# Order of the experts on TensorE, one more weight slot, one sum for the last pair and two store queues in a mixture-of-experts layer

## The chip, the core and the metric

The kernel runs on one core of a Trainium2 chip. Its time is the device time of one launch in microseconds (us), and less is better. Five engines share the core's memory: TensorE (PE in the profile, with PEld for loading the stationary operand), VectorE (DVE), ScalarE (ACT), GpSimd (POOL) and SyncE (SP). SP does no arithmetic here, it issues transfers. An engine takes its instructions in the order in which the program lists them, and waits at an instruction until what that one needs is there.

## The reference

One transformer layer on 512 tokens of width 1024, in float32: first `x + hybrid_mixer(rms_norm(x))` (a short convolution, a sparse attention and a gated delta rule, merged by gates), then `x + hier_moe(rms_norm(x))`. The change lies in the second half, whose core is:

```python
def hier_moe(h, w_rg, b_rg, w_re, b_re, w_eg, w_eu, w_ed):
    # a token takes the best of 4 groups, and in it the best 2 of 8 experts
    ...
    def expert_block(args):
        xb, e = args
        return (jax.nn.silu(xb @ w_eg[e]) * (xb @ w_eu[e])) @ w_ed[e]
    ...
    y = yb...[dest] * gate_s[:, None]
    return jax.ops.segment_sum(y, tok_s, num_segments=n_tok)
```

There are 32 experts with two matrices of 1024x512 (gate `w_eg`, up `w_eu`) and one of 512x1024 (down `w_ed`) each, 6.3 MB an expert and 201 MB in all. Every one is read once.

## The kernel before

The mixer, the router and the tables of tokens fill the first 687 us. The rest is the loop `for pair in range(16)` (line 1326), followed by the last expert's down products (lines 1360 to 1382) and a block under `tc.If(any_over > 0)` (line 1386) that runs only when an expert has more than 64 tokens; with this input it does no work.

**A pair** is the experts `pair` and `pair + 16`, with 64 token slots each. `gather` (line 1160) fetches the pair's 128 token rows by index into `xg`; `turned` (line 1114) transposes them on TensorE (`pxg`) and multiplies by the norm's gain on VectorE into `xT`. `ffn_up` (line 1182) makes the gate and up products of one expert side by side in one PSUM tile `pgu` (lines 1185, 1186); ScalarE and VectorE make the activation `act` from it, `turn` transposes that (`pt`, line 1204), and `ffn_down` (line 1222) makes the down products `pd` (line 1228). In every second expert of a pair, the transposes of the other are called in the middle of its products.

**What becomes of `pd`.** For the pairs 0, 1, 11, 12 and 13 (`by_rows`, line 1246) ScalarE copies it and GpSimd scatters it to `yrows` in memory; these rows are fetched during pair 14 (`fetch_rows`, into weight slots), summed and added to the result `x` (`add_rows`, line 1275). For the other pairs `y_parts` (line 1217) makes a rounded half on ScalarE and the rest on VectorE into `y`, and VectorE makes a 0/1 matrix `sel` from the token numbers (line 1213), behind `y_parts` in the program. `combine` lists eight steps, four blocks of 128 tokens by two halves of 512 columns. `combine_step` (line 1280) is `sel` times `y` for each expert of the pair into `pc` (line 1286) and an add into `x` on VectorE (line 1288). Up to four of these steps are called in each `ffn_up` of the next pair.

**Weights.** `wchunk` (line 1073) loads 1 MB chunks, twelve a pair (four for each `ffn_up`, two for each `ffn_down`), all on SP's queue and from the 19th on in program order. They go in turn through 18 slots: chunk n takes the slot of chunk n - 18 when that one's last reader is done. `fetch_rows` takes four slots in the same turn. The last expert's `w_ed` comes as three chunks of 384, 320 and 320 columns.

**The end.** After the last pair's first expert, `combine` is called for that expert alone and its eight steps are run (`combine_rest`, line 1361). Then, for each of the three pieces of columns, come the down products (line 1376), `y_parts`, four combine steps of one expert each, and four stores to the output on SP (`store`, line 1305), one for each block of 128 tokens. The products of the second piece are told to come behind the eight steps of the first expert, those of the third behind the first piece's steps.

**Order on the engines.** The program text is not the order of issue. The kernel is built with `schedule_with_timeline_sim=True`: a planner lists the instructions of each engine by readiness in its own simulated time, with the program's order as priority. `tc.issue_after(ins)` forces a place behind an instruction; `tc.keep_in_program_order` keeps the program's order among those that ask for it. What the planner lists is fixed; on the chip the engine keeps that order whatever comes late.

Of the kernel before, what the change touches and what calls it, by code (L numbers as in the profile page):

```python
# [11 lines left out]
F32 = mybir.dt.float32  # L12
# [8 lines left out]
P = 128  # L21
S = 512
D = 1024
# [5 lines left out]
CAP = 64  # L29
# [70 lines left out]
def kernel(ctx, tc, x, w_in, w_nat, w_small, w_gate, w_branch, w_out, cmp_w1, cmp_w2,  # L100
# [966 lines left out]
    gp = late.enter_context(tc.tile_pool(name="gather", bufs=1))  # L1067
    ep = late.enter_context(tc.tile_pool(name="experts", bufs=1))
    tc.swap_default_side()
    slots = wslots + [(lp, f"{n}{i}") for n in ("hTh", "hTl") for i in range(2)]  # L1070
    nslot, nsel, rows, todo = [0], [0], [], []

    def wchunk(shape, src):
# [10 lines left out]

    gain = PR("nffg")

    def pair_input():
        return gp.tile([P, KT, 2 * CAP], F32, tag="xT", name="xT", bufs=3)

    itab = pair_input().rearrange("p k s -> p (k s)")[:, 0:512].rearrange("p (j c) -> p j c", c=64)  # L1090
    for j, tab in enumerate(islots):
        (nc.scalar if j < 4 else G).dma_start(itab[:, j], tab.rearrange("(p e) c -> p (e c)", p=P))

# [17 lines left out]
                                op0=ALU.mult, op1=ALU.add)  # L1111
                G.tensor_scalar(out=toks[64 * a:64 * a + 64, h], in0=info[hs, :, 0], scalar1=4096.0, scalar2=None, op0=ALU.add)

    def turned(xg):
        xT = pair_input()
        for h in range(2):
            pt = ps_mm.tile([P, 4, P], F32, tag="mm", name="pxg")
            for k in range(4):
                T.transpose(pt[:, k], xg[:, 4 * h + k::KT], ident)
            V.tensor_tensor(out=xT[:, 4 * h:4 * h + 4], in0=pt,  # L1120
                            in1=gain[:, 4 * h:4 * h + 4].unsqueeze(2).to_broadcast([P, 4, P]), op=ALU.mult)
        return xT
# [31 lines left out]
        with tc.issue_after(gathered[0][1]):  # L1154
            tables()

    gathered, moved = [], []


    def gather(pair):  # L1160
# [21 lines left out]
    def ffn_up(xs, wg, wu, info, between=None):  # L1182
        pgu = mpsum("pgu")
        for k in range(KT):
            T.matmul(pgu[0:64], xs(k), wg(k), start=k == 0, stop=k == KT - 1)  # L1185
            ins = T.matmul(pgu[64:128], xs(k), wu(k), start=k == 0, stop=k == KT - 1)  # L1186
            if between and k == 3:
                between()
            if k % 4 == 3:
                combine_step()  # L1190
                combine_step()
        with tc.issue_after(ins.ins):
            rss, gsl = info()
        act = ep.tile([P, 512], F32, tag="act", name="act")
        qk = lambda ap: ap.rearrange("p (q k) -> p k q", k=4)
        at = act[64:128].rearrange("p (k q) -> p k q", k=4)
        A.activation(at, qk(pgu[0:64]), AF.Silu, scale=rss)  # L1197
        V.scalar_tensor_tensor(out=at, in0=qk(pgu[64:128]), scalar=gsl, in1=at, op0=ALU.mult, op1=ALU.mult)  # L1198
        aT = ep.tile([P, 4, CAP], F32, tag="aT", name="aT", bufs=2)

        def turn():
            pt = ps_e.tile([P, 4, CAP], F32, tag="pt", name="pt")
            for k in range(4):
                ins = T.transpose(pt[:, k], act[64:128, k * P:(k + 1) * P], ident[64:128, 64:128])
            V.tensor_copy(aT, pt)
            return ins.ins

        return turn, aT
# [13 lines left out]
    def ffn_down(aT, wd, tok, between=None, to=None):  # L1222
        pd = mpsum("pd")

        def products(ks):
            for k in ks:
                for a in range(2):
                    T.matmul(pd[64 * a:64 * a + 64], aT[:, k], wd(k, a), start=k == 0, stop=k == 3)  # L1228

        products((0, 1))  # L1230
        with tc.issue_after(between()) if between else ExitStack():
            products((2, 3))
        if to is not None:
            y = ep.tile([P, D], F32, tag="y", name="yd", bufs=2)[:, 0:512]
            A.copy(out=y, in_=pd)
            with tc.issue_after(moved[-1]) if moved else ExitStack():
                ins = G.indirect_dma_start(out=yrows, out_offset=bass.IndirectOffsetOnAxis(ap=to, axis=0), in_=y,
                                           in_offset=None, bounds_check=4 * S - 1, oob_is_err=False)
            moved.append(ins.ins)
            return  # L1240
        y = ep.tile([P, D], F32R, tag="y", name="y", bufs=2)
        for a in range(2):
            y_parts(y, halves[a], pd, a)
        rows.append((selection(tok), y))
# [56 lines left out]
    def weights_down(ed):  # L1301
        wd = [wchunk([P, 2, D], ed.rearrange("(p h k) n -> h p k n", p=P, k=2)[j]) for j in range(2)]
        return lambda k, a: wd[k // 2][:, k % 2, 512 * a:512 * a + 512]

    def store(cols):
        for t in range(NT):
            nc.sync.dma_start(out2[t][:, cols], x1p[t // 2][:, t % 2, cols])


    nbi = mp.tile([P, NEXP + 1], I32, name="nbi")  # L1310
# [15 lines left out]
    for pair in range(NEXP // 2):  # L1326
# [17 lines left out]
        for h in range(1 if pair == NEXP // 2 - 1 else 2):  # L1344
            ffn_down(up[h][1], weights_down(w_ed[pair + 16 * h]), toks[:, h, pair:pair + 1],
                     None if h else up[1][0], yix[:, h, pair:pair + 1] if pair in by_rows else None)
            if h == 0 and pair + 1 < NEXP // 2:
                inputs.append(turned(gathered[-1][0]))
            if (pair, h) == (4, 0):
                row_table()  # L1350
                counts()
            if pair == 14:
                fetch_rows(2 * h)
                fetch_rows(2 * h + 1)
        if rows:
            combine()
            rows.clear()

# [24 lines left out]


    any_over = nc.values_load(nbi[0:1, NEXP:NEXP + 1], min_val=0, max_val=NEXP * 8)
    with tc.If(any_over > 0):
        with tc.For_i(0, NEXP, 1) as ei:
            n_over = nc.values_load(nbi[0:1, bass.ds(ei, 1)], min_val=0, max_val=S // CAP - 1)
# [4 lines left out]
            with tc.For_i(0, n_over, 1):  # L1393
# [22 lines left out]
                turn, aT = ffn_up(lambda k: xT[:, k], *weights_up(one(w_eg), one(w_eu)), lambda: (rss, gsl))  # L1416
                turn()
                ffn_down(aT, weights_down(one(w_ed)), tok)
                combine()
                rows.clear()  # L1420
                combine_rest()
# [71 lines left out]
```

## Time and profile before

| | |
|---|---|
| median of 3 runs | 1186.48 us (1185.94 to 1189.7) |
| the profiled execution: its time | 1186.4 us |
| its span, first to last instruction | 1184.6 us |
| PE busy | 1105.1 us (93%) |
| DVE busy | 572.4 us (48%) |
| ACT busy | 332.6 us (28%) |
| POOL busy | 127.6 us (11%) |
| bytes moved by DMA | 271.63 MB, mean 229 GB/s |

Busy time is the time in which an engine had at least one instruction in work; PE's is a modelled figure, and a busy PE is not a PE at its peak. All times in the rows below are from the first instruction of the span. A float32 matmul of this kernel stands in the trace as two instructions, so an `ffn_up` shows as 32 and an `ffn_down` as 16.

### The profile page before, as it was taken

To read this page: it belongs to the slowest core of one execution; us is meant where nothing else is said; L and a number is where in the kernel's file an instruction comes from. 1 tells how busy PE (TensorE), PEld (TensorE's weight loads), DVE (VectorE), ACT (ScalarE), POOL (GpSimd) and SP (SyncE) were. 2 spreads that over 40 slices of the span, in tenths; PEclk is the share of its full clock that TensorE was granted. 3 is DMA by queue.
4 is the path that set the end of the run, shared out by engine and by line. 5 is a ranking of instruction groups with operands and counts; after the bars stand their busy time and mean duration, and the time that the engine had idled before them with its cause. 6 is when DMAs were issued, how large, how long until landed. Compare 5 with 4: busy or idle time off the path is not lost.

```text
span 1184.6 us, 15574 instructions
## 1 busy us (share of the span) xinstructions
PE 1105.1 (93%) x5987; PEld 704.0 (59%) x5988; DVE 572.4 (48%) x1290; ACT 332.6 (28%) x678; POOL 127.6 (11%) x202
## 2 busy tenths in 40 slices
PE   0899999999999999999999999999998988899995
PEld 0788788987788887766789833333333333233332
DVE  1587486587644585566354521235343333221146
ACT  1443333343323445567332411111111001110110
POOL 3100130420000000000000151200000000011260
PEclk9899999999999999999999999999999999999997
DMA  8122233312222222100586569999999999999992
GB/s 337 58 90 94 84 107 108 108 54 81 80 72 83 89 72 89 48 25 1 211 322 263 196 261 418 418 418 418 419 419 419 419 419 412 395 380 418 407 382 76
DMA packets 52862, 271.63 MB, mean 229 GB/s; under 512 B 8586, under 2 KB 12554, under 8 KB 27952
## 3 DMA queue, kind: packets, MB, share of 16 engines
q1 hardware_dynamic: 44928, 254.95, 55.1%
q0 software_dynamic: 5280, 11.31, 2.5%
q10 hardware_dynamic: 2576, 4.32, 1.1%
q8 instruction: 49, 0.80, 0.3%
q14 instruction: 29, 0.24, 0.1%
HBM read 267.25 MB, written 11.29 MB: 235 GB/s over the span
## 4 chain that ended last, share of the span: by engine, by line
PE 65%; issue 25%; DMA 4%; DVE 2%; POOL 2%; ACT 1%; POOLq 0%; ACTq 0%; DVEq 0%
PE pmm L189 9%; PE pmm L187 9%; PE pmm L188 8%; PE pgu L1185 5%; PE pd L1228 3%; PE po L838 2%; PE pb L187 2%; PE pb L188 2%; DMA yrows<-zero 2%; PE pb L189 2%; DMA yrows<-yd,yix 2%; PE ptp L821 2%; PE pmn L556 1%; PE pgu L1186 1%; PE pmn L555 1%
## 5 line engine op out<-in xcount | busy, mean ns | idle before, releaser
L1185 PE MATMUL pgu<-we,xT 128*64 128x512 f32 x512 | 238.2, 610 | 1.9 <-DVE xT L1120 1.1
L1186 PE MATMUL pgu<-we,xT 128*64 128x512 f32 x512 | 236.5, 610 | 0.0
L189 PE MATMUL pmm<-hTh,lo 128*128 128x512 f32 x432 | 172.2, 399 | 0.2 <-DVE lo L182 0.2
L187 PE MATMUL pmm<-hTh,hi 128*128 128x512 f32 x432 | 171.1, 396 | 0.3 <-DVE fa L704 0.3
L188 PE MATMUL pmm<-hTl,hi 128*128 128x512 f32 x432 | 170.4, 394 | 0.0
L182 DVE TENSOR_TENSOR lo<-raw,hi 128x1024 fp32r<-128x1024 f32 x82 | 100.3, 1223 | 112.5 <-ACT hi L181 111.2
L181 ACT CAST hi<-raw 128x1024 fp32r<-128x1024 f32 x82 | 86.1, 1050 | 168.4 <-PE pmm L188 94.1
L1228 PE MATMUL pd<-we,aT 128*64 128x512 f32 x496 | 120.9, 599 | 1.6 <-issue 1.1
L1185 PEld LDWEIGHTS pgu<-we,xT 128*64 128x64 f32 x512 | 67.3, 139 | 81.4 <-issue 77.9
L1288 DVE TENSOR_TENSOR x<-pc,x 128x512 f32<-128x512 f32 (+2 forms) x100 | 62.8, 665 | 87.5 <-PE pc L1286 86.9
L1186 PEld LDWEIGHTS pgu<-we,xT 128*64 128x64 f32 x512 | 66.3, 139 | 63.7 <-issue 60.9
L1197 ACT ACTIVATE act<-pgu,rg 64x512 f32<-64x512 f32 x32 | 21.8, 681 | 277.1 <-PE pgu L1186 184.2
L189 PEld LDWEIGHTS pmm<-hTh,lo 128*128 128x128 f32 x432 | 81.3, 188 | 18.7 <-DVE lo L182 1.8
L187 PEld LDWEIGHTS pmm<-hTh,hi 128*128 128x128 f32 x432 | 81.6, 189 | 17.0 <-DVE fa L704 0.8
L188 PEld LDWEIGHTS pmm<-hTl,hi 128*128 128x128 f32 x432 | 81.5, 189 | 16.5
L1286 PE MATMUL pc<-y,sel 128*128 128x512 f32 (+2 forms) x180 | 59.8, 438 | 27.9 <-DVE sel L1213 22.5
L1286 PEld LDWEIGHTS pc<-y,sel 128*128 128x128 f32 x180 | 30.5, 193 | 72.0 <-issue 46.3
L1228 PEld LDWEIGHTS pd<-we,aT 128*64 128x64 f32 x496 | 35.2, 136 | 59.2 <-issue 55.0
L1198 DVE SCALAR_TENSOR_TENSOR act<-pgu,rg,act 64x512 f32<-64x512 f32 x32 | 24.2, 756 | 89.7 <-ACT act L1197 89.2
L1220 DVE TENSOR_TENSOR y<-pd,y 64x512 fp32r<-64x512 f32 (+2 forms) x48 | 30.9, 644 | 61.9 <-ACT y L1219 61.7
L1219 ACT CAST y<-pd 64x512 fp32r<-64x512 f32 (+2 forms) x48 | 26.1, 544 | 116.9 <-PE pd L1228 74.8
L187 PE MATMUL pb<-yhi,hi 128*128 128x512 f32 x96 | 37.6, 397 | 1.3 <-ACT yhi L536 1.3
(796 smaller groups left out, 1729.7 us busy)
## 6 DMA issues: line engine op xcount, KB each, us to landing
we<-in_w_eg_dram SPq DMA_DIRECT2D x64, 1024.0 KB, 19.9
we<-in_w_eu_dram SPq DMA_DIRECT2D x64, 1024.0 KB, 19.9
we<-in_w_ed_dram SPq DMA_DIRECT2D x62, 1024.0 KB, 19.9
raw<-in_w_in_dram SPq DMA_DIRECT2D x30, 512.0 KB, 3.6
raw<-in_w_gate_dram SPq DMA_DIRECT2D x24, 512.0 KB, 3.5
raw<-in_w_branch_dram SPq DMA_DIRECT2D x12, 512.0 KB, 3.5
yrows<-zero POOLq DMA_DIRECT2D x1, 4096.0 KB, 21.7
raw<-in_w_nat_dram SPq DMA_DIRECT2D x8, 512.0 KB, 3.7
```

The costliest lines, as they stand in the source:

```text
L181: A.copy(out=hi, in_=raw)
L182: V.tensor_tensor(out=lo, in0=raw, in1=hi.bitcast(F32), op=ALU.subtract)
L187: T.matmul(ps, ahi(k), bhi(k), start=start and k == 0, stop=False)
L188: T.matmul(ps, ahi(k), blo(k), start=False, stop=False)
L189: T.matmul(ps, alo(k), bhi(k), start=False, stop=stop and k == n - 1)
L1185: T.matmul(pgu[0:64], xs(k), wg(k), start=k == 0, stop=k == KT - 1)
L1186: ins = T.matmul(pgu[64:128], xs(k), wu(k), start=k == 0, stop=k == KT - 1)
L1219: A.copy(out=y[hi, cols], in_=pd[hi])
L1220: V.tensor_tensor(out=y[lo, cols], in0=pd[hi], in1=y[hi, cols].bitcast(F32), op=ALU.subtract)
L1228: T.matmul(pd[64 * a:64 * a + 64], aT[:, k], wd(k, a), start=k == 0, stop=k == 3)
L1286: ins = T.matmul(pc[:, 0:n], sel[:, t * P:(t + 1) * P], y[:, cols], start=i == 0, stop=i == len(src) - 1)
L1288: V.tensor_tensor(out=xo, in0=pc[:, 0:n], in1=xo, op=ALU.add)
```

## The change

Four things are changed, and three smaller ones make room for them.

1. In `ffn_up` the gate and up products are issued behind `downs[-1]`, the last down product of the pair before. `ffn_down` records that instruction.
2. A 19th slot `es9` of 8 KB a partition is added to the list of weight slots. Its space comes from `xT`, which had three buffers: the even pairs now have one buffer, and the odd pairs' `xT` takes turns with `xg` in the two buffers `raw`. The table `itab`, read once at the start, moves from an `xT` buffer to one of the two `y` buffers.
3. `combine` is called in the loop only when both experts of a pair are listed. The last pair's first expert stays in the list, so that the combine steps of the three pieces each take both experts into one `pc`; the eight steps of the first expert alone are gone, and so is the order behind them.
4. `store` makes two transfers a piece instead of four, each of 256 token rows, one on SP's and one on ScalarE's queue.

```diff
-    slots = wslots + [(lp, f"{n}{i}") for n in ("hTh", "hTl") for i in range(2)]
+    slots = wslots + [(lp, f"{n}{i}") for n in ("hTh", "hTl") for i in range(2)] + [(gp, "es9")]
...
-    def pair_input():
-        return gp.tile([P, KT, 2 * CAP], F32, tag="xT", name="xT", bufs=3)
-
-    itab = pair_input().rearrange("p k s -> p (k s)")[:, 0:512].rearrange("p (j c) -> p j c", c=64)
+    def pair_input(pair=0):
+        if pair % 2:
+            return ringa.tile([P, KT, 2 * CAP], F32, tag="raw", name="xT", bufs=2)
+        return gp.tile([P, KT, 2 * CAP], F32, tag="xT", name="xT")
+
+    itab = ep.tile([P, D], F32, tag="y", name="itab", bufs=2)[:, 0:512].rearrange("p (j c) -> p j c", c=64)
...
         for k in range(KT):
-            T.matmul(pgu[0:64], xs(k), wg(k), start=k == 0, stop=k == KT - 1)
-            ins = T.matmul(pgu[64:128], xs(k), wu(k), start=k == 0, stop=k == KT - 1)
+            with tc.issue_after(downs[-1]) if downs else ExitStack():
+                T.matmul(pgu[0:64], xs(k), wg(k), start=k == 0, stop=k == KT - 1)
+                ins = T.matmul(pgu[64:128], xs(k), wu(k), start=k == 0, stop=k == KT - 1)
...
         with tc.issue_after(between()) if between else ExitStack():
-            products((2, 3))
+            downs.append(products((2, 3)))
...
     def store(cols):
-        for t in range(NT):
-            nc.sync.dma_start(out2[t][:, cols], x1p[t // 2][:, t % 2, cols])
+        for i, q in enumerate((nc.sync, nc.scalar)):
+            q.dma_start(out.rearrange("(i t p) d -> i p t d", p=P, t=2)[i][:, :, cols], x1p[i][:, :, cols])
...
-        if rows:
+        if len(rows) == 2:
             combine()
             rows.clear()
```

`turned` gets the pair's number to pick the buffer, and `downs` is cleared around the block that does not run.

## Rows read from the trace of the kernel before

**Rows 1.** The page's second part: the span in 40 equal slices of 29.6 us. The line is what the DMA engines moved in each, in GB/s.
```profile
GB/s 337 58 90 94 84 107 108 108 54 81 80 72 83 89 72 89 48 25 1 211 322 263 196 261 418 418 418 418 419 419 419 419 419 412 395 380 418 407 382 76
```
**Rows 2.** Busy time by stretch. The columns are: stretch in us, its length, then for PE, PEld, DVE, ACT and POOL the busy us and the instructions, then the granted clock, the DMA share and GB/s.
```profile
687.00:762.00 75.00, 72.15 (x354) 29.43 (x353) 13.72 (x28) 8.16 (x13) 21.43 (x35) 1.00 0.95 381
785.00:905.00 120.00, 119.68 (x523) 45.56 (x523) 53.34 (x94) 14.04 (x23) 5.05 (x5) 1.00 1.01 419
905.00:1051.00 146.00, 127.35 (x516) 47.07 (x514) 49.84 (x80) 14.83 (x25) 1.98 (x2) 0.96 1.00 407
...
1132.00:1158.00 26.00, 25.84 (x104) 8.91 (x106) 11.36 (x17) 1.36 (x2) 13.61 (x9) 0.93 0.86 329
1158.00:1178.20 20.20, 12.79 (x70) 7.59 (x66) 16.21 (x32) 2.93 (x8) 0.00 (x0) 0.79 0.22 79
```
**Rows 3.** TensorE in order of time, from the down products of pair 1 to the first up products of pair 2, and the first down products of pair 2: start, length, line, operation, count, and in brackets the idle time before it and what ended that.
```profile
729.21 1.94 PE L1228 MATMUL pd<-we,aT 128*64 128x512 f32 x8 [0.56 <-issue]
...
738.37 0.61 PE L1185 MATMUL pgu<-we,xT 128*64 128x512 f32 x1 [0.44 <-issue]
...
753.29 1.08 PE L1228 MATMUL pd<-we,aT 128*64 128x512 f32 x4 [0.56 <-issue]
```
**Rows 4.** TensorE and VectorE in order of time around the down products of pair 10 and the first up products of pair 11, in the same columns.
```profile
1021.85 0.48 DVE L1213 TENSOR_SCALAR sel<-c_moe,toks 128x512 fp32r<-128x512 f32 x1
1022.49 0.93 PE L1286 MATMUL pc<-y,sel 128*128 128x512 f32 x3 [1.67 <-DVE sel L1213]
...
1028.04 0.49 DVE L1213 TENSOR_SCALAR sel<-c_moe,toks 128x512 fp32r<-128x512 f32 x1
1028.67 0.94 PE L1286 MATMUL pc<-y,sel 128*128 128x512 f32 x3 [2.53 <-DVE sel L1213]
...
1030.14 1.06 PE L1186 MATMUL pgu<-we,xT 128*64 128x512 f32 x1
```
**Rows 5.** TensorE in order of time: the first down products of the pairs 3, 7 and 11.
```profile
785.20 0.65 PE L1228 MATMUL pd<-we,aT 128*64 128x512 f32 x2
...
905.01 1.03 PE L1228 MATMUL pd<-we,aT 128*64 128x512 f32 x4
...
1050.64 0.60 PE L1228 MATMUL pd<-we,aT 128*64 128x512 f32 x2
```
**Rows 6.** What TensorE waited for between 762 and 1060 us: us in total, times, longest.
```profile
PE pc L1286 <- DVE sel L1213: 18.9, 9, 2.5
```
**Rows 7.** TensorE in order of time: in pair 3, up products of pair 4 ahead of the second expert's down products; the first down products of pair 12; the first up products of pair 14, and the first down products of the pairs 13 and 14.
```profile
793.30 1.45 PE L1185 MATMUL pgu<-we,xT 128*64 128x512 f32 x3
794.16 0.64 PE L1228 MATMUL pd<-we,aT 128*64 128x512 f32 x1
...
1073.14 0.59 PE L1228 MATMUL pd<-we,aT 128*64 128x512 f32 x1
...
1098.77 0.61 PE L1185 MATMUL pgu<-we,xT 128*64 128x512 f32 x1
...
1104.80 1.92 PE L1228 MATMUL pd<-we,aT 128*64 128x512 f32 x8
...
1120.55 1.89 PE L1228 MATMUL pd<-we,aT 128*64 128x512 f32 x8
```
**Rows 8.** SP's queue. First two issues in order of time (start, length of the group, line, what, count), then two of its waits late in the loop (us in total, times, longest), then the median time of a weight chunk from issue to landing (last column) with its size.
```profile
1092.70 6.94 SPq L1079 DMA_DIRECT2D we<-in_w_ed_dram  x4
1115.02 0.33 SPq L1079 DMA_DIRECT2D we<-in_w_eg_dram  x1
...
SPq L1079 <- PE pd L1228: 13.2, 1, 13.2
...
SPq L1079 <- DVE x L1275: 11.3, 1, 11.3
...
we<-in_w_eg_dram SPq DMA_DIRECT2D x64, 1024.0 KB, 19.9
```
**Rows 9.** Busy time by stretch, in the columns of the second group: the idle queue before the loop, and the stretch from the first reuse of a slot to the end of the last pair's products.
```profile
685.00:691.00 6.00, 4.78 (x27) 2.29 (x28) 1.98 (x3) 0.00 (x0) 4.60 (x5) 1.00 0.08 15
691.00:1158.00 467.00, 439.80 (x1936) 167.20 (x1934) 150.91 (x253) 50.81 (x82) 63.12 (x79) 0.99 1.00 406
```
**Rows 10.** The end, from 1158 us. First a group by line and shape (count, busy us, mean ns, idle before it), then single rows in order of time, then the output transfers of 160 KB with their median us from issue to landing.
```profile
L1288 DVE TENSOR_TENSOR x<-pc,x 128x512 f32<-128x512 f32 x8 | 5.0, 681 | 0.0
...
1157.90 1.47 PE L1376 MATMUL pd<-we,aT 128*64 128x192 f32 x16
1162.12 1.23 DVE L1275 TENSOR_TENSOR x<-yr,x 128x1024 f32<-128x1024 f32 x1
1167.63 2.36 PE L1376 MATMUL pd<-we,aT 128*64 128x160 f32 x16
1176.40 1.71 DVE L1288 TENSOR_TENSOR x<-pc,x 128x320 f32<-128x320 f32 x4 [0.51 <-PE pc L1286]
...
out_dram<-x SPq DMA_DIRECT2D x8, 160.0 KB, 2.3
```
**Rows 11.** What the moved buffers touch: the last table instruction that reads `itab`, the second copy of pair 0's down products, and the gathers with their median us from issue to landing.
```profile
711.71 0.27 POOL L1112 TENSOR_SCALAR toks<-info 64x16 f32<-64x16 f32 x1
...
712.81 0.58 ACT L1235 COPY yd<-pd 128x512 f32<-128x512 f32 x1 [2.85 <-PE pd L1228]
...
xg<-x1rows,tix POOLq DMA_INDIRECT x15, 8.5
```

More of the change, by code (lines that the diff above doesn't have):

```diff
@@ L1112, in tables, with turned @@
                 G.tensor_scalar(out=toks[64 * a:64 * a + 64, h], in0=info[hs, :, 0], scalar1=4096.0, scalar2=None, op0=ALU.add)
-    def turned(xg):
-        xT = pair_input()
+    def turned(xg, pair=0):
+        xT = pair_input(pair)
         for h in range(2):
@@ L1155, in first_info @@
             tables()
-    gathered, moved = [], []
+    gathered, moved, downs = [], [], []
     def gather(pair):
@@ L1227, in products @@
                 for a in range(2):
-                    T.matmul(pd[64 * a:64 * a + 64], aT[:, k], wd(k, a), start=k == 0, stop=k == 3)
+                    ins = T.matmul(pd[64 * a:64 * a + 64], aT[:, k], wd(k, a), start=k == 0, stop=k == 3)
+            return ins.ins
         products((0, 1))
         with tc.issue_after(between()) if between else ExitStack():
-            products((2, 3))
+            downs.append(products((2, 3)))
         if to is not None:
@@ L1347 @@
             if h == 0 and pair + 1 < NEXP // 2:
-                inputs.append(turned(gathered[-1][0]))
+                inputs.append(turned(gathered[-1][0], pair + 1))
             if (pair, h) == (4, 0):
@@ L1385 @@
     any_over = nc.values_load(nbi[0:1, NEXP:NEXP + 1], min_val=0, max_val=NEXP * 8)
+    downs.clear()
     with tc.If(any_over > 0):
@@ L1418 @@
                 ffn_down(aT, weights_down(one(w_ed)), tok)
+                downs.clear()
                 combine()
```

## The prediction

> **What bounds the kernel now.** I read the slices of the span first. In the last third the weights stream at 418 to 419 GB/s in most slices, with dips to 395, 380, 407 and 382 [rows 1]. This looks like a loop bound by its transfers, and the table by stretch says that this is only half of it. From 785 to 905 us TensorE is busy for 119.68 of 120 us beside 419 GB/s, so both run full. From 905 to 1051 us TensorE is busy for only 127.35 of 146 us, at a mean clock of 0.96, and the transfers fall to 407 GB/s [rows 2]. The engine that idles there doesn't wait for weights. Of its waits, 18.9 us in nine times end with `sel` from VectorE, before the combine products `pc` [rows 6].
>
> The order of time shows how. In pair 10 TensorE stands 1.67 us before three `pc` products and then 2.53 us before three more, each time until VectorE has made `sel` behind the `y` parts; then up products take 1.06 us [rows 4] where they take 0.59 us at full clock [rows 7]. The planner put `pc` early because in its time no weights were there; on the chip they were, and the listed order made TensorE wait.
>
> The price of that pattern is read from the first down products of the pairs 3, 7 and 11: (905.01 - 785.20) / 4 = 29.95 us a pair without it, (1050.64 - 905.01) / 4 = 36.41 us with it [rows 5], so 6.4 us a pair, four pairs, 25.8 us. The transfers give the floor: 467 us at 406 GB/s is 189.6 MB [rows 9], at 419 GB/s 452.5 us, so about 1143.5 us for the last weights instead of 1158. Up to 14 us are to be had in the loop, no more.
>
> Behind 1158 us VectorE is the engine that counts: busy for 16.21 of 20.2 us [rows 2]. Then come 6.4 us of stores and the end of the program, and 1.8 us outside the span (1186.4 less 1184.6). The profiled execution stands 0.1 us below the median, so the sum is made against 1184.6 and 1.8 us are added.
>
> **The tail.** The eight adds of 512 columns for the last pair's first expert go: 5.0 us of VectorE [rows 10]. With them goes the wait of the second piece's products: its matmuls ran at 1167.63, although TensorE had finished the first piece's at about 1159.4 [rows 10]. That wait lies beside VectorE's work, so I count the 5.0 us once. The last piece's chunk had waited 11.3 us for a slot held by fetched rows until `add_rows` (L1275) had read them [rows 8]. With 19 slots it takes the slot of a down chunk of pair 14. Its products come in the program behind the first piece's combine steps, so after 1167.63 [rows 10], and nothing is saved there; but the slot also let `add_rows` run late, and one of its adds, 1.23 us, stands in the tail at 1162.12 [rows 10]. With its row fetch earlier in the turn it runs before: 1.2 us. Against this, each piece's first add now waits for two products instead of one: 0.51 us stood before the last piece's first add [rows 10], so some 0.2 us more for three pieces, 0.6 us. Sum: -5.0 - 1.2 + 0.6 = -5.6 us. If the 4.0 us that VectorE idles in this stretch [rows 2] go too, it is -9; if the add stays and the new order brings stalls of two waits of 0.5 us, -3.
>
> The stores: a transfer of 160 KB lands 2.3 us after its issue [rows 10]. The last one is now 320 KB; at 419 GB/s the second half is 0.4 us, and two issues less in SP's queue give about as much back. ScalarE's queue now waits at a store for the adds of a piece, with the casts of the next piece possibly behind it; those adds take 1.71 us [rows 10]. Between -0.5 and +1.7 us I take 0, since the planner has the casts ready earlier.
>
> **The 19th slot.** SP's queue stood idle from 685 to 691 us (15 GB/s) before the first slot was given back [rows 9]. One chunk more, 1.05 MB or 2.5 us at 419 GB/s, is loaded in that hole. Directly it saves 2.5 us only where transfers set the end, and they don't in the first place. Indirectly it moves the point at which the plan runs out of weights: pairs cost 29.95 us on TensorE and 12.6 MB / 419 GB/s = 30.0 us in transfers, nearly the same, so a lead of 2.5 us lasts long. I take one pair of the four that leaves the pattern: -6.4 us. The bounds are 0 and the floor above, -14.
>
> **The order.** Most pairs are in order already: in pair 1 the ups of the next pair start at 738.37, behind all downs, and the pairs 1 and 2 are 753.29 - 729.21 = 24.1 us apart with 0.5 us of waits at each change [rows 3]. Out of order are pair 3, where ups of pair 4 run before the second expert's downs, and pair 14, whose ups start at 1098.77, before pair 13's first downs at 1104.80 [rows 7]. The latter held SP for 13.2 us, with the issues of weights standing from 1099.6 to 1115.02 [rows 8]; but chunks land 19.9 us after their issue [rows 8], so the queue covers most of it, and TensorE at this place is behind its weights anyway. For TensorE itself the two pairs to 14 took 1120.55 - 1073.14 = 47.4 us [rows 7] and take 2 x 24.1 = 48.2 in order: +0.8 us. What could be lost: two pairs (3 and another like it) in which the planner, forbidden to take ups, puts `pc` into the hole and so makes the pattern of pair 10: 2 x 6.4 = +12.9 us. What could be won is in the bound of -14 above. I take +0.8.
>
> **The moved buffers.** `itab` was read for the last time at 711.98 and the copy that now needs its buffer began at 712.81 [rows 11]: 0.8 us to spare, and behind it PSUM's second `pd` buffer, so 0. A gather now waits for the ups of the pair whose `xT` it replaces, which is most of a pair's 30 us [rows 5] later than before, and has another 30 us until it is turned; it takes 8.5 us [rows 11]: 0. Without that cover it would cost its landing, 8.5 us, once a pair.
>
> **Sum.** 1184.6 - 5.6 - 6.4 + 0.8 = 1173.4 us of span, with 1.8 us 1175.2 us: -1.0%.
>
> **Rivals.** *Transfers set the end.* If in-order release removes the pattern in all four pairs, TensorE would be 25.8 us ahead, and the floor holds: -14 - 5.6 gives 1165.0, with 1.8 us 1166.8 us. For it: SP's 13.2 us behind out-of-order downs [rows 8]. Against it: the pairs 7 to 10 have the pattern while being almost in order (`ffn_down` of pair 10 ends before pair 11's ups [rows 4]). One thing more speaks against it: a TensorE that really waits for each chunk idles oftener, and after 2.53 us of idling the up products of rows 4 ran at 1.06 us, half the clock. [...] So I give this rival 0.22 and not 0.30.
>
> *The pattern spreads (slower).* In the planner's time weights are late from pair 3 on. Before, it filled two holes with ups of the next pair; forbidden that, it lists `pc` products there, and TensorE on the chip waits for `sel` in pairs that ran 29.95 us. Two pairs: 1184.6 - 5.6 + 0.8 + 12.9 = 1192.7, with 1.8 us 1194.5 us. From one pair on (+6.4) the tail's gain is used up. For it: the idle 0.3 us of 120 in 785 to 905 [rows 2], that is, nothing there can get better and something can get worse. Against it: the 19th slot.
>
> *Only the tail counts.* The loop's order changes without a gain: 1184.6 - 5.6 + 0.8 + 1.8 = 1181.6 us, and with a stall at ScalarE's stores up to 1184.
>
> **How the numbers follow.** Chances: the forecast (1170 to 1181) 0.40, transfers set the end 0.22, only the tail 0.18, the pattern spreads 0.20. What this kernel's timing can tell from no change is 0.3%, 3.6 us: faster is below 1182.9, slower above 1190.0. Faster: 0.40 + 0.22 + two thirds of the third = 0.74, less 0.04 for a cost that I don't see: 0.70. Same: the rest of the third, a third of the spreading and 0.01 of the unseen cost, 0.14. Slower: the rest of the spreading and 0.03, 0.16. The range goes from 1163, the floor with the tail at -9, to 1194, the pattern in two more pairs; the likeliest case alone is 1170 to 1181.
>
> **What would show it.** Right: adds of L1288 behind the last pair fall from 20 to 12, and the time from the end of the last pair's first downs to the last add from 20.2 to about 14.6 us; waits `pc` for `sel` fall from 18.9 to about 14; the pairs 3 to 6 stay at 30 us. The first rival: 419 GB/s in every slice up to the last, and TensorE waiting for weights. The second: gaps before `pc` in the pairs 3 to 6. I am wrong if the first downs of pair 11 come later than 1051 us, or if ScalarE's casts in the tail wait behind stores.

## The result and the profile after

The changed kernel takes 1174.99 us (median of 4 runs, 1174.33 to 1176.75) against 1188.09 us (1185.94 to 1192.69) of the kernel before on the same chip. The ratio is 0.9899, with a 95% interval of 0.9872 to 0.9927. The prediction was 1175.2 us. The profiled execution of after took 1175.39 us, with a span of 1173.6 us; the rows below are of that one. Behind the changed lines all line numbers move up by three or four: the up products are L1188 and L1189, the down products L1231, `sel` L1216, `pc` L1290 and its add L1292.

First the slices of after, GB/s of the DMA engines. The dips to 395, 380 and 407 of [rows 1] are gone; only the last two slices lie under 417.

```profile
GB/s 340 59 90 92 88 108 110 109 55 73 90 56 100 90 54 90 54 37 1 167 304 332 128 290 417 418 418 419 419 419 419 420 419 418 419 419 419 418 383 96
```

Then busy time by stretch of after, in the columns of [rows 2].

```profile
785.00:905.00 120.00, 119.15 (x510) 43.36 (x506) 49.78 (x89) 14.74 (x24) 5.22 (x11) 1.00 1.01 419
905.00:1051.00 146.00, 139.12 (x593) 51.00 (x593) 54.10 (x86) 15.91 (x26) 6.39 (x7) 0.98 1.01 419
1051.00:1105.00 54.00, 49.80 (x240) 19.61 (x237) 7.96 (x13) 5.75 (x9) 12.24 (x10) 1.00 1.01 419
1105.00:1132.00 27.00, 20.80 (x88) 6.86 (x90) 8.64 (x11) 3.00 (x5) 15.87 (x12) 0.98 1.02 415
1132.00:1158.00 26.00, 23.87 (x114) 9.54 (x111) 14.66 (x21) 3.10 (x6) 2.35 (x1) 0.95 0.50 187
```

From 905 to 1051 us TensorE now works for 139.12 us where [rows 2] had 127.35. But from 1105 to 1132 us it works for only 20.80 of 27 us beside transfers at 415 GB/s, where before it worked for 25.00:

```profile
1105.00:1132.00 27.00, 25.00 (x122) 9.20 (x118) 7.12 (x13) 4.85 (x8) 13.89 (x11) 1.00 1.01 407
```

The idle time has moved to the end of the loop. The places of the pairs show the same. These are TensorE's first down products of the pairs 3, 7 and 11 in after, and those of the last expert's first piece.

```profile
784.26 1.94 PE L1231 MATMUL pd<-we,aT 128*64 128x512 f32 x8
...
905.08 1.94 PE L1231 MATMUL pd<-we,aT 128*64 128x512 f32 x8
...
1033.51 0.59 PE L1231 MATMUL pd<-we,aT 128*64 128x512 f32 x1
...
1152.85 1.47 PE L1380 MATMUL pd<-we,aT 128*64 128x192 f32 x16
```

The pairs 3 to 6 are as before, (905.08 - 784.26) / 4 = 30.2 us each. The pairs 7 to 10 take (1033.51 - 905.08) / 4 = 32.1 us instead of 36.4 [rows 5], so TensorE reaches pair 11 17.1 us earlier than before. At the last expert it is only 1157.90 - 1152.85 = 5.05 us earlier [rows 10]. 12 us were won and lost again in between. The waits of TensorE in after, from 700 to 1180 us (us in total, times, longest), name most of what it lost them to.

```profile
PE pc L1290 <- DVE sel L1216: 8.2, 4, 2.1
PE pgu L1189 <- DMA we<-in_w_eu_dram: 6.3, 3, 2.7
PE pd L1380 <- DVE y L1223: 2.1, 1, 2.1
...
PE pgu L1188 <- DMA we<-in_w_eg_dram: 1.2, 1, 1.2
```

Waits for `sel` fell from 18.9 us [rows 6] to 8.2. Waits for the weights of the up products came in their place, 7.5 us, and another 0.8 us for the weights of down products; all of them lie between 1102 and 1130 us. So weights account for 8.3 of the 12 us; the rest was not itemised. At the end, the rows of after in order of time are these.

```profile
1154.45 1.23 DVE L1279 TENSOR_TENSOR x<-yr,x 128x1024 f32<-128x1024 f32 x1
...
1156.46 1.31 PE L1380 MATMUL pd<-we,aT 128*64 128x160 f32 x16 [2.13 <-DVE y L1223]
...
1161.44 0.40 ACTq L1311 DMA_DIRECT2D out_dram<-x  x1
1161.88 0.29 ACT L1222 CAST y<-pd 64x160 fp32r<-64x160 f32 x1 [2.77 <-PE pc L1290]
...
1164.99 1.68 DVE L1292 TENSOR_TENSOR x<-pc,x 128x320 f32<-128x320 f32 x4 [0.51 <-PE pc L1290]
```

The last add ends at 1164.99 + 1.68 = 1166.67 us, 13.8 us behind the start of the last expert's products; before it was 20.2 (1157.90 to 1178.11). From there to the end it takes 6.9 us instead of 6.5 (1184.6 less 1178.11). The busy times of after in this stretch, in the columns of [rows 2]:

```profile
1152.85:1166.67 13.82, 10.05 (x74) 6.76 (x70) 10.98 (x23) 2.94 (x8) 0.00 (x0) 1.00 0.28 104
```

VectorE is busy for 10.98 us and idle for 2.8, where it was busy for 16.21 and idle for 4.0 [rows 2]. The second piece's products start at 1156.46, 3.6 us behind the first piece's; before it was 1167.63 less 1157.90, 9.7 us [rows 10].

### The profile page after: what moved, and what is told of

Its sections match the earlier page's. It is cut to its first block, busy times and chain, and to the rows that moved or that the text cites. A ratio compares the mean times of both kernels' runs of the same rounds, so it can differ in the third digit from the quotient of the medians.

```text
span 1173.6 us, 15577 instructions
## 1 busy us (share of the span) xinstructions
PE 1101.4 (94%) x5991; PEld 699.2 (60%) x5992; DVE 570.0 (49%) x1282; ACT 332.7 (28%) x678; POOL 127.3 (11%) x202
## 4 chain that ended last, share of the span: by engine, by line
PE 83%; DMA 8%; issue 4%; DVE 2%; ACT 1%; POOL 1%; POOLq 0%; ACTq 0%; DVEq 0%; SPq 0%
PE pgu L1188 9%; PE pmm L189 9%; PE pmm L187 9%; PE pmm L188 9%; PE pd L1231 7%; PE pgu L1189 6%; PE pc L1290 4%; DMA we<-in_w_eu_dram 4%; PE po L838 2%; PE pb L187 2%; PE pb L188 2%; DMA yrows<-zero 2%; PE pb L189 2%; DMA yrows<-yd,yix 2%; PE ptp L821 2%
## 5 line engine op out<-in xcount | busy, mean ns | idle before, releaser
L1189 PE MATMUL pgu<-we,xT 128*64 128x512 f32 x512 | 235.5, 607 | 6.3 <-DMA we<-in_w_eu_dram 6.3
L1188 PE MATMUL pgu<-we,xT 128*64 128x512 f32 x512 | 237.0, 607 | 4.4 <-DVE xT L1122 2.1
L1188 PEld LDWEIGHTS pgu<-we,xT 128*64 128x64 f32 x512 | 66.5, 139 | 96.3 <-issue 88.2
L1231 PE MATMUL pd<-we,aT 128*64 128x512 f32 x496 | 114.9, 599 | 4.0 <-issue 1.7
L1292 DVE TENSOR_TENSOR x<-pc,x 128x512 f32<-128x512 f32 (+2 forms) x92 | 59.1, 665 | 104.6 <-PE pc L1290 104.1
L1189 PEld LDWEIGHTS pgu<-we,xT 128*64 128x64 f32 x512 | 64.8, 139 | 57.1 <-issue 46.4
L1290 PE MATMUL pc<-y,sel 128*128 128x512 f32 (+2 forms) x184 | 62.4, 431 | 9.3 <-DVE sel L1216 8.2
L1231 PEld LDWEIGHTS pd<-we,aT 128*64 128x64 f32 x496 | 33.2, 136 | 61.0 <-issue 52.7
L1290 PEld LDWEIGHTS pc<-y,sel 128*128 128x128 f32 x184 | 29.7, 188 | 54.1 <-issue 30.9
L1168 POOL DMA_INDIRECT xg<-x1rows,tix x15 | 15.3, 1018 | 257.4 <-PE pxg L1121 107.9
```

The source lines that it names most:

```text
L1231: ins = T.matmul(pd[64 * a:64 * a + 64], aT[:, k], wd(k, a), start=k == 0, stop=k == 3)
L1290: ins = T.matmul(pc[:, 0:n], sel[:, t * P:(t + 1) * P], y[:, cols], start=i == 0, stop=i == len(src) - 1)
L1292: V.tensor_tensor(out=xo, in0=pc[:, 0:n], in1=xo, op=ALU.add)
```

## The experiments

Three questions were open. Which part brings how much? Which part made the loop denser? And what became of the 12 us? The first four runs undo one part of the change each, on one chip with a kernel before at 1185.67 us there. Of the next four, three put one part into the kernel before (1185.85 us) and one makes an edit that stands in neither kernel. The last four (1186.04 us) take transfers or waits away. The changed kernel itself was not run again beside them, so where a run is compared with its 1174.99 us, the two times come from different chips. The kernel before agrees within 0.4 us on the three chips of the experiments, over 15 to 29 runs each; differences of 1 to 2 us from 1174.99 are therefore not resolved.

**The order undone.**

```diff
-            with tc.issue_after(downs[-1]) if downs else ExitStack():
+            with ExitStack():
```

> The changed kernel without the order of the up products (the rest as changed). Theory A (the order makes the loop denser: it keeps the planner from running ups ahead of downs, and slots come free in the order of the queue): the first downs of pair 11 come at 1045 us or later instead of 1033.5, TensorE waits for sel for 15 us or more in 762 to 1060 us, and the time rises by 5 to 10 us to 1180 to 1185. Theory B (the 19th slot alone made the loop denser): within 2 us of the changed kernel's 1175.0, the first downs of pair 11 at 1033 to 1036. Theory C (in the changed kernel the weights set the end, so that TensorE's earlier arrival is lost at the end anyway): pair 11 later by some us, but the time within 2 us.

Measured: 1176.43 us, ratio 0.9921 (0.9902 to 0.9941). Pair 11 is reached at 1035.66 us, so the order is not what made the loop denser:

```profile
1035.66 0.59 PE L1231 MATMUL pd<-we,aT 128*64 128x512 f32 x1
```

The numbers are those of Theory B, but the next run shows that the slot was not the cause either. The loss against 1174.99 is 1.4 us, and the intervals overlap: its price alone isn't resolved. The down products of pair 13 are behind the ups of pair 14 again, and SP's queue, from 1020 to 1160 us, waits for `pd` once more (10.3 us), which it does for 0.2 us in after; its one wait for `pc` grows from 5.2 to 10.8 us:

```profile
SPq L1079 <- PE pc L1290: 10.8, 1, 10.8
SPq L1079 <- PE pd L1231: 10.3, 4, 5.6
```

**18 slots, with the moved buffers left as they are.**

```diff
-    ... for n in ("hTh", "hTl") for i in range(2)] + [(gp, "es9")]
+    ... for n in ("hTh", "hTl") for i in range(2)]
```

> The changed kernel without the slot es9 (18 slots; xT and itab stay in their new buffers). Theory A (order): the loop up to pair 11 hardly moves (first downs at 1033 to 1038), transfers stay at 418 to 419 GB/s, and the time rises by at most 2.5 us, one chunk less ahead. Theory B (slot): the pattern of waits for sel comes back, pair 11 at 1045 or later, 5 to 10 us more. If the weights set the end (theory C), the rise is the 2.5 us of one chunk, and more if the last chunk waits for add_rows again.

Measured: 1177.58 us (1176.9 to 1178.85), ratio 0.9927 (0.991 to 0.9945), 2.6 us above 1174.99. The intervals of the two ratios just overlap, but the lowest of these runs lies above the highest of after (1176.75). Pair 11 is reached at 1031.12 us: the loop is as dense without the slot.

```profile
1031.12 1.89 PE L1231 MATMUL pd<-we,aT 128*64 128x512 f32 x8
```

TensorE's waits for the weights of the up products between 1020 and 1140 us grow from 6.3 and 1.2 us to these:

```profile
PE pgu L1189 <- DMA we<-in_w_eu_dram: 11.0, 7, 3.0
PE pgu L1188 <- DMA we<-in_w_eg_dram: 1.6, 1, 1.6
```

So the slot is worth about the transfer of one chunk, 2.5 us, and nothing by the order of the list. Neither the order nor the slot made the loop denser, which no theory here had foreseen; the moved buffers, which both runs keep, are left.

**The last pair's first expert added alone again.**

```diff
-        if len(rows) == 2:
+        if rows:
```

> The changed kernel with the last pair's first expert combined alone again (eight adds of 512 columns and the order behind them are back; the rest as changed). My prediction's term: 5.0 us for the adds, 5 to 6.5 us in all, so 1180 to 1181.5. Rival (the adds lay beside the wait for the last weights): less than 2 us.

Measured: 1182.33 us, ratio 0.9968 (0.9956 to 0.998), 7.3 us above 1174.99. In the groups by line and shape from 1152 us on, the eight adds of 512 columns are back, 5.0 us:

```profile
L1292 DVE TENSOR_TENSOR x<-pc,x 128x512 f32<-128x512 f32 x8 | 5.0, 684 | 0.2 <-PE pc L1290 0.2
```

In order of time, the last adds end at 1171.59 + 2.16 = 1173.75 us, 20.7 us behind the last expert's first products at 1153.09:

```profile
1171.59 2.16 DVE L1292 TENSOR_TENSOR x<-pc,x 128x320 f32<-128x320 f32 x5
```

**Four stores a piece again, on SP's queue.**

```diff
-        for i, q in enumerate((nc.sync, nc.scalar)):
-            q.dma_start(out.rearrange("(i t p) d -> i p t d", p=P, t=2)[i][:, :, cols], x1p[i][:, :, cols])
+        for t in range(NT):
+            nc.sync.dma_start(out2[t][:, cols], x1p[t // 2][:, t % 2, cols])
```

> The changed kernel with four stores a piece on SP's queue again. From the last add to the end the changed kernel has 6.9 us, the kernel before 6.4. If the two larger transfers cost what that says, this one is 0.3 to 0.8 us faster; if the queue of four issues costs 0.5 us, it is as much slower; in both cases within 1 us of 1175.0.

Measured: 1175.07 us, ratio 0.9904 (0.9885 to 0.9923): no difference that the runs resolve. The larger transfers land later (320 KB in 2.7 and 3.4 us, 160 KB in 2.3 [rows 10]) and fewer stand in a queue.

**The moved buffers alone, in the kernel before.**

```diff
-    def pair_input():
-        return gp.tile([P, KT, 2 * CAP], F32, tag="xT", name="xT", bufs=3)
...
+    def pair_input(pair=0):
+        if pair % 2:
+            return ringa.tile([P, KT, 2 * CAP], F32, tag="raw", name="xT", bufs=2)
+        return gp.tile([P, KT, 2 * CAP], F32, tag="xT", name="xT")
...
+    itab = ep.tile([P, D], F32, tag="y", name="itab", bufs=2)[:, 0:512].rearrange("p (j c) -> p j c", c=64)
```

> The kernel before with the moved buffers alone (xT of the odd pairs in turn with the gathered rows, the index table in a y buffer); 18 slots, no new order, old end, four stores. Theory A (the moved buffers are what changed the listed order of the loop): the combine products are listed between the ups, the first downs of pair 11 come at 1031 to 1037 us, pc waits for sel for under 10 us; but the last weights land within 2 us of before, so the time is only 1183 to 1187. Theory B (the prediction: the buffers cost and bring nothing): first downs of pair 11 at 1050, about 19 us of waits for sel, time as before.

Measured: 1186.9 us, ratio 1.0012 (1.0001 to 1.0023). TensorE reaches pair 11 at 1031.68 us, 19 us before [rows 5], and the last expert only half a microsecond before [rows 10]:

```profile
1031.68 1.89 PE L1231 MATMUL pd<-we,aT 128*64 128x512 f32 x8
...
1157.36 1.49 PE L1380 MATMUL pd<-we,aT 128*64 128x192 f32 x16
```

Theory A holds for pair 11 and for the time. The moved buffers are the part that changes the listed order of the pairs 7 to 10, and that order is worth nothing at the end. The waits for `sel` fell less than expected, to 12.9 us, and waits for weights came instead. From 700 to 1180 us:

```profile
PE pc L1290 <- DVE sel L1216: 12.9, 6, 2.7
PE pgu L1188 <- DMA we<-in_w_eg_dram: 8.6, 2, 7.2
PE pgu L1189 <- DMA we<-in_w_eu_dram: 3.1, 3, 1.9
```

**The order alone, in the kernel before.**

```diff
+            with tc.issue_after(downs[-1]) if downs else ExitStack():
...
+            downs.append(products((2, 3)))
```

> The kernel before with the gate and up products behind the last down product of the pair before, nothing else. Theory A (the order is not what made the loop denser): the pairs 7 to 10 stay at 36 us each, pair 11 at 1050 to 1056, time 1184 to 1189. Theory B (the prediction's price of 0.8 us plus its slower rival, the waits spread to two more pairs): pair 7 later than 911 and time over 1191. Theory C (the order releases the weights sooner): pair 11 before 1040, time under 1182.

Measured: 1187.53 us, ratio 1.0015 (1.0005 to 1.0026), slightly slower. Pair 7 starts its downs at 906.34 and pair 11 at 1053.85 us, so the pattern stays in four pairs at 36.9 us each and doesn't spread:

```profile
906.34 1.89 PE L1229 MATMUL pd<-we,aT 128*64 128x512 f32 x8
...
1053.85 1.89 PE L1229 MATMUL pd<-we,aT 128*64 128x512 f32 x8
```

That is Theory A. Put into the kernel before, the order costs 1.7 us; in the changed kernel it costs nothing that shows, for undoing it lost 1.4 us (not resolved).

**The combine products behind the ups, in the kernel before.** This edit stands in neither kernel. It takes the early place of `pc` out of the list directly.

```diff
             if k % 4 == 3:
-                combine_step()
-                combine_step()
+                with tc.issue_after(ins.ins):
+                    combine_step()
+                    combine_step()
```

> The kernel before with one edit that is in neither kernel: each pair of combine steps is issued behind the up product after which it is called. Theory A (the early place of the combine products in the list is the whole of the 6.4 us a pair, whatever put them there): pairs 7 to 10 at 30 us each, pair 11 at 1028 to 1035, waits for sel under 3 us, and the time 1181 to 1186, because TensorE then waits for weights that land within 4 us of before. Theory B (what is saved in the loop arrives at the end): 1168 to 1172. Theory C (the waits for sel only stood in for waits for weights): pair 11 at 1045 or later, with waits for weights instead.

Measured: 1185.83 us, ratio 1.0 (0.9989 to 1.0011). The pairs 7 to 10 take (1019.03 - 904.44) / 4 = 28.6 us each, less than expected, and TensorE is 31.6 us ahead at pair 11; the time doesn't move. That is Theory A. In order of time:

```profile
904.44 1.94 PE L1229 MATMUL pd<-we,aT 128*64 128x512 f32 x8
...
1019.03 1.94 PE L1229 MATMUL pd<-we,aT 128*64 128x512 f32 x8
...
1155.91 1.47 PE L1377 MATMUL pd<-we,aT 128*64 128x192 f32 x16
```

At the last expert 2.0 us are left of the 31.6. Where the other 29.6 went is in the waits of TensorE from 1020 to 1140 us, 15.9 us for weights:

```profile
PE pgu L1185 <- DMA we<-in_w_eg_dram: 8.9, 2, 4.7
PE pgu L1186 <- DMA we<-in_w_eu_dram: 7.0, 5, 2.6
```

and in the granted clock, the third number from the end in these rows of busy time by stretch:

```profile
1051.00:1105.00 54.00, 41.41 (x164) 13.50 (x164) 5.60 (x9) 3.80 (x6) 4.05 (x4) 0.87 1.01 419
1105.00:1132.00 27.00, 24.16 (x105) 8.32 (x101) 6.62 (x11) 3.59 (x6) 17.02 (x14) 0.87 0.99 401
```

A clock of 0.87 over these 81 us is at most 0.13 x 81 = 10.5 us of work, for the mean is taken over the waits too. So waits for weights and the lower clock account for up to 26 of the 29.6 us.

**The joint sum alone, in the kernel before.**

```diff
-        if rows:
+        if len(rows) == 2:
```

> The kernel before with the joint sum of the last pair's experts alone. The prediction's term: 5.6 us less, 1180.1. By the run that undid this part in the changed kernel: 7.3 us less, 1178.4. Rival (the eight adds lay beside other work when the loop ends late): under 3 us less, 1183 or more. The first downs of pair 11 stay at 1050.

Measured: 1178.9 us, ratio 0.9944 (0.993 to 0.9957): 7.0 us less, as its undoing cost 7.3. The first downs of pair 11 stay, at 1050.83 us. The end runs from the last expert's first products at 1158.76 us to the last add's 1170.88 + 1.28 = 1172.16, 13.4 us. This one condition gives more than half of what the whole change gives.

**Four chunks less to load, in after, in the kernel with `pc` behind the ups, and in before.** The up weights of pair 12 are left out and its gate weights are used in their place: TensorE does as many products, but these kernels no longer compute the layer and serve for their time alone. The number of chunks that keep the program's order falls by the same four.

```diff
-        gu = [wchunk(...) for j in range(2) for w in (eg, eu)]
-        return lambda k: gu[k // 4 * 2][:, k % 4], lambda k: gu[k // 4 * 2 + 1][:, k % 4]
+        gu = [wchunk(...) for j in range(2) for w in (eg, eu) if w is not None]
+        n = len(gu) // 2
+        return lambda k: gu[k // 4 * n][:, k % 4], lambda k: gu[k // 4 * n + n - 1][:, k % 4]
...
-            up.append(ffn_up(..., *weights_up(w_eg[e], w_eu[e]), ...))
+            up.append(ffn_up(..., *weights_up(w_eg[e], None if pair == 12 else w_eu[e]), ...))
```

> The changed kernel without the four chunks of w_eu of pair 12 (its gate weights are used in their place, so TensorE does the same products); 4.2 MB or 10 us of transfers less, behind the stretch in which the two lists differ. Theory A (with the loop dense, TensorE waits for weights at 1103 to 1130 and transfers set the end): these waits go, 5 to 9 us less than the changed kernel, 1166 to 1170. Theory B (TensorE's own work sets the end): at most 2 us less, 1173 or more.

> The kernel before with the combine products behind the ups (the loop dense, first downs of pair 11 at 1019 us, time as before), without the four chunks of w_eu of pair 12, as in the run beside it. Theory A (what the dense loop gains is given back to waits for weights behind 1035 us): 8 to 10 us less, 1176 to 1178. Theory B (something behind the loop sets the end, whatever the weights do): 1184 or more.

> The kernel before without the four chunks of w_eu of pair 12; the waits for sel in the pairs 7 to 10 stay. Theory A (before, TensorE's late loop and the transfers come out at nearly the same end, so that taking away either one alone brings little): 0 to 3 us less, 1183 to 1186. Theory B (before was bound by its transfers already): 8 to 10 us less, 1176 to 1178.

Measured: after falls to 1164.71 us (ratio 0.9817, 0.9802 to 0.9832), 10.3 us below 1174.99. The kernel with `pc` behind the ups falls to 1175.21 us (0.9903, 0.9888 to 0.9919), 10.6 us below 1185.83. The kernel before falls to 1184.17 us (0.9992, 0.9975 to 1.0008), which can't be told from no change. For the first two this is more than Theory A had (5 to 9 and 8 to 10 us), for the third it is Theory A. In after without the chunks TensorE waits for no weights of the up products from 1020 to 1140 us, and from 1105 to 1132 us it works for 26.20 instead of 20.80 us; the row of that stretch:

```profile
1105.00:1132.00 27.00, 26.20 (x114) 9.17 (x114) 10.54 (x16) 3.68 (x6) 16.78 (x12) 1.00 0.98 393
```

4.2 MB at 419 GB/s are 10.0 us. Both kernels with a dense loop give back all of it, so their transfers set the end. In the one with `pc` behind the ups TensorE still waits for weights from 700 to 1180 us, about as long as with the chunks:

```profile
PE pgu L1185 <- DMA we<-in_w_eg_dram: 11.8, 3, 7.1
PE pgu L1186 <- DMA we<-in_w_eu_dram: 3.6, 3, 1.8
```

So there transfers set the pace even with 10 us less of them (this profiled execution took 1178.12 us, above its median). In before without the chunks the waits for `sel` from 700 to 1180 us stay, and the last expert starts at 1155.20 instead of 1157.90 us. Its row in the waits:

```profile
PE pc L1286 <- DVE sel L1213: 21.1, 10, 2.5
```

Here the transfers could not use the 10 us. From 1105 to 1115 us they nearly stood (136 and 24 GB/s in its two halves), for SP's queue waited for down products before it could issue the next chunks. The queue's row from 1020 to 1160 us:

```profile
SPq L1079 <- PE pd L1228: 33.7, 11, 17.2
```

Before, then, TensorE's late loop and the transfers ended within some 2 us of each other. Taking away the waits alone gave 0.0 us, taking away 10 us of transfers alone 1.9 by the medians (not resolved), both together 10.6.

**The rest of the waits for `sel` taken away, in after.** `sel` is made ahead of the `y` parts, and `pc` is issued behind the ups as above.

```diff
+        sel = selection(tok)
         for a in range(2):
             y_parts(y, halves[a], pd, a)
-        rows.append((selection(tok), y))
+        rows.append((sel, y))
```

> The changed kernel with sel made ahead of the y parts and the combine products behind the ups after which they are called, to take away the waits for sel that are left (8.2 us in four times). Theory A (behind 1100 us the weights set the pace): the waits for sel fall under 2 us, the waits for weights grow by about as much, and the time is 1173 to 1176. Theory B (these waits are on the path): 5 to 8 us less, 1167 to 1170.

Measured: 1175.45 us, ratio 0.9911 (0.9897 to 0.9924): no difference from after. The waits for `sel` are gone, but the waits for weights didn't grow, as Theory A had it. TensorE stands before the first up products of a pair instead, with no releaser named by the profile. Its waits from 700 to 1180 us:

```profile
PE pgu L1188 <- issue: 11.0, 7, 2.5
```

It reaches the first downs of pair 11 at 1049.07 us:

```profile
1049.07 1.94 PE L1232 MATMUL pd<-we,aT 128*64 128x512 f32 x8
```

So the loop was not made denser by this, and what holds these products is open. It is one more case of the same: the first downs of pair 11 came 15.6 us later than in after, and the time is the same. A part of the 15.6 us can be another place of these products in the list: counted by TensorE's instructions in the trace from 905 to 1051 us, this kernel lies between the two, with 555 against 593 in after and 516 before.

No version here that loads all weights beats the changed kernel by more than the runs differ.

## Why the prediction was right, and where its steps were wrong

The time came out within 0.2 us, and that close it was by luck. The slot was priced 3.8 us too high, the tail 1.4 to 1.7 us too low, and the order, where undone, had the other sign by 2.2 us (not resolved): the errors cancel, -11.2 us predicted against 11.4 lost in the four runs that undo a part each. The mechanism behind the largest term was wrong.

| step | predicted | measured |
|---|---|---|
| the tail | -5.6 | -7.0 put in alone, 7.3 lost when undone |
| the 19th slot | -6.4 | 2.6 lost when undone |
| the order | +0.8 | +1.7 put in alone, 1.4 lost when undone (not resolved) |
| the moved buffers | 0 | +1.0 put in alone; pair 11 19 us earlier |
| the stores | 0 | 0.1 lost when undone |

*The tail.* The eight adds were 5.0 us, as predicted (the row of the run that puts them back), and the adds behind the last pair fell from 20 to 12. The step "1.2 us" for `add_rows` failed: its last add still stands in the tail, at 1154.45 us. What made the term larger is VectorE's idle time, 4.0 us before and 2.8 after, of which the bound of -9 took all and the sum nothing: the second piece's products come 6.1 us sooner behind the first piece's, although they now wait 2.13 us for `y`. Before, VectorE stood 1.72 us at this place, until the second piece's `y` was there:

```profile
1170.36 0.32 DVE L1220 TENSOR_TENSOR y<-pd,y 64x160 fp32r<-64x160 f32 x1 [1.72 <-ACT y L1219]
```

The products of that piece took 2.36 us [rows 10], at a granted clock of 0.54 from 1167.63 to 1169.99 us (0.79 in the whole tail [rows 2]); in after they take 1.31 us, at 1.00. No term of the sum had the clock of the tail. The time from the last expert's first products to the last add was to be 14.6 us and is 13.8. The casts did come to stand behind a store on ScalarE's queue (1161.88 behind 1161.44, ScalarE idle for 2.77 us before it), which I had named as a sign of being wrong; the run with four stores, where ScalarE's queue has no store, takes the same time.

*The 19th slot.* This is the step that failed: "one pair of the four that leaves the pattern: -6.4 us". The price was 2.6 us. The slot takes no pair out of the pattern. All four pairs lost most of it, by the moved buffers, and that would have been worth 17.1 us if the lead at pair 11 reached the end. So the waits for `sel` fell to 8.2 us and not to about 14. The sentence "Directly it saves 2.5 us only where transfers set the end, and they don't in the first place" is where I went wrong: with the loop dense they do, and 2.5 us is what it gives. The 25.8 us that I priced for the pattern are, if anything, too few as time that TensorE loses (the run with `pc` behind the ups wins 31.6 us at pair 11), and wrong as time of the kernel, since the transfers end only a little earlier. In that run closing these gaps moved the kernel's time by 0.0 us, as long as the transfers stayed.

*The floor.* "Up to 14 us" was too much. It took the whole stretch from 691 to 1158 us at 419 GB/s, but behind 1132 us the rate of 329 GB/s [rows 2] was for the most part transfers running out and not transfers held up: (419 - 329) / 419 x 26 = 5.6 us. In stretches of 5 us from 1140 us on it was 416, 372, 250 and 15 GB/s; held up was the last chunk of 640 KB, which waited 11.3 us for its slot [rows 8]. The first 94 us were slow in both kernels (406 and 410 GB/s). What could be won was 146 x 12 / 419 = 4.2 us from 905 to 1051 us and under 1 us in each of the two stretches behind it (413 and 407 GB/s). And TensorE has work behind the last up weights: in the run with `pc` behind the ups the last wait for weights ends at 1135.68 us, and the last expert starts at 1155.91.

*The moved buffers.* I asked what they wait for and costed that at 0, rightly. I did not ask what they do to the listed order. With the odd pairs' `xT` in turn with the gathered rows, the planner puts the transposes of the next pair behind the down products and spreads `pc` between the ups. Why its simulated time comes out so is not settled; that the early `pc` is the cause of TensorE's waits for `sel` is shown by the run that moves `pc` alone.

*The rivals.* "Transfers set the end" is the right mechanism with the wrong floor: it named waits for weights and 419 GB/s in every slice up to the last, and both are there, 8.3 us of waits and 417 to 420 GB/s from the 25th slice up to the last two. It took the half clock for a reason against itself; in after too the granted clock fell to 0.50, from 1131.46 to 1134.50 us, and the transfers set the end all the same. In the run with `pc` behind the ups, TensorE's rows from 1067 us on show waits and clock together:

```profile
1067.33 1.94 PE L1185 MATMUL pgu<-we,xT 128*64 128x512 f32 x2 [4.74 <-DMA we<-in_w_eg_dram]
1070.52 1.12 PE L1186 MATMUL pgu<-we,xT 128*64 128x512 f32 x1 [1.25 <-DMA we<-in_w_eu_dram]
...
1071.43 1.06 PE L1186 MATMUL pgu<-we,xT 128*64 128x512 f32 x1
...
1073.68 0.59 PE L1186 MATMUL pgu<-we,xT 128*64 128x512 f32 x1
```

After 4.74 us of idling the up products take 1.06 to 1.12 us, at a granted clock of 0.50 from 1067.3 to 1073.1 us, and 0.59 us again from 1073.68. "The pattern spreads" fell: alone, the order left the pairs 3 to 6 nearly as they were (pair 7 at 906.34 instead of 905.01 us). "Only the tail counts" is nearest to the share of the parts: 7 of 11 to 13 us.

## What to carry to other kernels

A stall of the busiest engine is worth its length only up to the next limit, and in this case that limit was some 2 us away: take the stall and the transfers away each alone and then together, as the run with `pc` behind the ups and the three with fewer chunks do, before one is called the bound. A floor from transfers counts the work that must follow the last transfer, and leaves out the stretch in which they merely run out. And where a planner lists the instructions, a buffer shared in another way is a change of order, to be read from the listed order and not from the waits for that buffer alone.

## What the runs showed that I had not expected

In the run with `pc` behind the ups TensorE is 31.6 us ahead of its former place and loses it not by waiting alone: behind the waits for weights it works at a lower granted clock, 0.87 in the mean from 1051 to 1132 us, and up products take 1.06 us there where they take 0.59 at 1.00. In after too the clock is lower behind such waits, though later and for a shorter time. Its granted clock is 1.00 from 1051 to 1105 us, with its first wait for weights, 2.75 us, only at the end of that stretch, and 0.66 from 1130 to 1135 us, behind waits of 1.16, 1.74 and 1.79 us:

```profile
1129.69 0.64 PE L1189 MATMUL pgu<-we,xT 128*64 128x512 f32 x1 [1.79 <-DMA we<-in_w_eu_dram]
...
1131.46 1.12 PE L1189 MATMUL pgu<-we,xT 128*64 128x512 f32 x1
```

In two of the runs the sum of the waits doesn't tell what they cost in clock. With 18 slots TensorE waits for the weights of up products for 12.6 us from 1020 to 1140 us, at most 3.0 us at a time, and the granted clock is 1.00 from 1051 to 1132 us; with `pc` behind the ups it waits for 15.9 us, 4.74 and 4.16 us of it at a time, and the clock is 0.87. What of a wait decides was not tried.
